# A table of position bias: eight copies of 128 rows within DRAM in place of one transfer from SBUF

## The chip, the cores and the metric

The kernel runs on one core of a Trainium2 chip. The core has a matrix engine (TensorE, PE in the profile), a vector engine (VectorE, DVE), an engine for activations and copies (ScalarE, ACT), a general one (GpSimd, POOL) and an engine that issues the transfers (SyncE, SP). Each engine works through its own list of instructions strictly in order and waits at an instruction until what it needs is there. Transfers between DRAM and the on-chip SBUF run on 16 DMA engines, behind the instruction that issues them.

The metric is the device time of one execution in microseconds. Three runs of the kernel before took 1793.67, 1798.79 and 1799.83 us; the median is 1798.79 us.

## The reference

Five layers run one after another on 512 tokens of width 1024: a latent attention (MLA), a sliding-window attention (SWA), an attention with forget gates (FOX), a second MLA, and then a block of another kind with four mixers, a feed-forward part and a gate. Only two places matter here. The last block adds a learned bias to the attention scores of eight heads, and that bias depends only on the distance between the two tokens:

```python
bias_tab[:, rel_bucket(tq[:, None] - spos[None, :])]     # 8 heads, 32 buckets, distances 0 to 511
```

And the second layer, SWA, is where the kernel happens to prepare it:

```python
x = first_block(...)          # layers MLA, SWA, FOX, MLA
x = second_block(x, ..., rel_bias_2, ...)
```

## The kernel before

Every matrix product is done in three passes over operands that are split into a high and a low part. A weight block comes from DRAM into a raw tile (`wr`, six buffers), ACT rounds it to the high part (`wh`, line 137), POOL subtracts to get the low part (`wl`, line 138), and PE multiplies with both (lines 156 to 158). A raw buffer is free for the next load when POOL has read it. All transfers are issued by SP, in one queue.

Inside one layer the work goes over pairs of heads. For each pair, `prep` projects queries and keys into PSUM banks (`ps_acc`, three of them), ACT and DVE split these into parts (line 225 to 227 for keys, 202 and 203 for queries) and so free the bank, and then two heads are scored, exponentiated and multiplied with the values. The second layer starts with a projection of its values, one gate, then keys and queries of the first pair together (`proj_multi`, 96 matmuls of 256 columns), then the next projection.

A scheduler sets the order of the instructions on each engine from the program and a model of their times. An instruction that is written late but has all that it needs can come to stand earlier in its engine's list.

Right behind the first layer, `rel_rows` makes a table of the bias: a one-hot matrix times the bias table gives one row of 640 numbers for each of the 8 heads (512 distances and a masked tail), in SBUF, on 8 partitions. Line 792 writes every row 128 times into a DRAM tensor `rel` of 8 x 128 x 640 numbers. Much later, in the last block, `rel_bias` (line 798) reads one head's 128 rows with a step of 639 numbers, so that each partition gets the row shifted by one: this turns a function of distance into a 128 x 512 bias tile. The first of these loads is issued at 1096.3 us.

Of the kernel before, what the change touches and what calls it, by code (L numbers as in the profile page):

```python
# [9 lines left out]
F32 = mybir.dt.float32  # L10
# [5 lines left out]
P, S, D, T = 128, 512, 1024, 4  # L16
# [59 lines left out]
class Act:  # L76


    def __init__(s, hi, lo, n):
        s.hi, s.lo, s.n = hi, lo, n  # L80
# [8 lines left out]
class Kern:  # L89
    def __init__(s, ctx, tc, I, C):  # L90
        s.tc, s.nc, s.I, s.C = tc, tc.nc, I, C
        s.ctx = ctx
        s.sb = ctx.enter_context(tc.tile_pool(name="sb", bufs=1))
        s.dram = ctx.enter_context(tc.tile_pool(name="dram", bufs=1, space=bass.MemoryType.DRAM))
        s.phase_pool, s.phase_tags = None, {}
        s.ps = ctx.enter_context(tc.tile_pool(name="ps", bufs=1, space=PSUM))
        nc = s.nc
        s.ident = s.const("c_ident")
        s.small = s.sb.tile([P, 8], F32, name="small")
        nc.vector.memset(s.small[:, 0:4], -0.5)  # L100
        nc.vector.memset(s.small[:, 4:5], 1e-6)
        nc.vector.memset(s.small[:, 5:6], 1.0)
        s.x = []
        s.step = 48

    def const(s, name, dt=F32):
# [538 lines left out]
    def swa(s, j, li, xT, g_next):  # L645
        nc, I = s.nc, s.I
        Win, Wo = I["swa_w_in"][j], I["swa_w_out"][j]
        sinks = s.bcast_row(I["swa_sinks"][j], "gq")
        vt = [s.t(g, [P, T, 2, 2, 64], R, name="v") for g in ("ckv", "cq")]
        s.v_proj(Win, 1280, 256, xT, lambda t, ps: s.v_split(ps, [v[:, t] for v in vt]))  # L650
        oT = s.act(8)
        K = {}

        def prep(p):
            kp, pr = divmod(p, 4)
            if p == 0:
                kps, qps = s.proj_multi([(Win, 1024, P, "acc"), (Win, 0, P, "acc")], xT)
            else:
                kps = s.proj(Win, 1024 + kp * P, P, xT) if pr == 0 else None
                qps = None  # L660
            if pr == 0:
                K[kp] = s.split_k(kps)
            win = s.t("rope", [P, 2, 256], name="win")
            nc.sync.dma_start(win, s.C["c_win"][p])
            qt = s.split_q(qps or s.proj(Win, p * P, P, xT))
            return qt, [k[:, pr // 2] for k in K[kp]], win

        def head(d, p, e):
            hd = 2 * p + e
            q, (kd, kl), win = d  # L670
            return s.attend(lambda out, i, k0: s.qk_mm(out, i, k0, q, e, kd, kl), [0, 0, 1, 2],
                            lambda i: win[:, e, 128:] if i == 0 else win[:, e], 0.125, s.vsel(vt[p // 4], (p % 4) // 2),
                            sink=sinks[:, hd:hd + 1])

        s.pairs(range(8), prep, head, Win, 1536, xT, oT)
        return s.layer_end(Wo, oT, li, g_next)

# [101 lines left out]
    def rel_rows(s):  # L779

        nc = s.nc
        hot = s.t("p", [32, S])
        nc.sync.dma_start(hot, s.C["c_hot"])
        tab = s.t("f", [32, 8])
        nc.sync.dma_start(tab, s.I["rel_bias_2"].rearrange("h b -> b h"))
        s.rel = s.dram.tile([8, P, 640], F32, name="rel")
        r = s.t("p", [8, 640])
        ps = s.p("acc")
        nc.tensor.matmul(ps[:8], tab, hot, start=True, stop=True)
        nc.vector.memset(r[:, 512:], NEG)  # L790
        nc.scalar.mul(r[:, :512], ps[:8], 8.0)
        nc.sync.dma_start(s.rel, r.rearrange("h (o c) -> h o c", o=1).to_broadcast([8, P, 640]))

    def rel_bias(s, h):


        b = s.t("rb", [P, S])
        s.nc.sync.dma_start(b, bass.AP(tensor=s.rel.tensor, offset=s.rel.offset + h * P * 640 + 127,
                                       ap=[[639, P], [1, S]]))
        return b  # L800

    def conv(s, W, hT, mix, b):
# [326 lines left out]
```

## Time and profile before

| | |
|---|---|
| median of three runs | 1798.79 us |
| the profiled execution | 1800.88 us |
| its span, first to last instruction | 1799.1 us |
| TensorE busy | 1695.6 us (94% of the span) |
| VectorE, ScalarE, GpSimd busy | 959.6, 873.9, 853.9 us |
| mean granted TensorE clock | 0.975 |
| share of the DMA engines' time in use | 34.7% |

The profile comes from one execution. The time of that execution is 1.8 us longer than its span, and 2.1 us above the median of the three runs. The engines' busy times overlap, so they do not add up to the span. The first layer ends and the second begins at about 275 us; the second ends at about 500 us.

### The profile page before, as it was taken

How to read it: one execution, taken by the hardware profiler on the slowest of the kernel's cores; microseconds unless marked ns; L12 is line 12 of the kernel's file. 1: busy time of each engine (PE TensorE's matmuls, PEld its weight loads, DVE VectorE, ACT ScalarE, POOL GpSimd, SP SyncE). 2: the span in 40 equal slices, each digit the busy share in tenths (PEclk: the TensorE clock that was granted, in tenths of full speed). 3: DMA queues.
4: the chain of work that ended last, by engine and by line, in shares of the span. 5: the costliest groups of instructions: out<-in, count | busy, mean ns of one | idle time of the engine just before them, and what ended most of it. 6: DMA issues, size and time to landing. Idle time of an engine off the chain costs nothing.

```text
span 1799.1 us, 25682 instructions
## 1 busy us (share of the span) xinstructions
PE 1695.6 (94%) x8818; PEld 1429.8 (79%) x8818; DVE 959.6 (53%) x2223; ACT 873.9 (49%) x2054; POOL 853.9 (47%) x775
## 2 busy tenths in 40 slices
PE   8999999499899999999999998999999999999999
PEld 7888778377788888877888777877788888888877
DVE  4587643278763575576477667499545222210054
ACT  4566533366635565662466653654544333332252
POOL 1645433234345565645644424635744444444571
PEclk9999999699899999999999999999999999999999
DMA  5534534422224233423354522332322333332321
GB/s 166 132 94 118 166 90 56 115 81 71 61 55 118 79 80 83 116 85 118 96 131 100 158 86 58 94 89 59 111 90 81 94 94 94 94 95 87 100 99 71
DMA packets 190203, 173.89 MB, mean 97 GB/s; under 512 B 14152, under 2 KB 154824, under 8 KB 190072
## 3 DMA queue, kind: packets, MB, share of 16 engines
q1 hardware_dynamic: 190072, 172.25, 34.7%
q8 instruction: 70, 1.15, 0.3%
q14 instruction: 61, 0.50, 0.1%
HBM read 148.31 MB, written 6.85 MB: 86 GB/s over the span
## 4 chain that ended last, share of the span: by engine, by line
PE 51%; DVE 9%; ACT 3%; POOL 2%; issue 2%; DMA 1%; SPq 0%; ACTq 0%; POOLq 0%; DVEq 0%
PE ps_acc L156 11%; PE ps_acc L157 10%; PE ps_acc L158 10%; PE ps_s L156 4%; PE ps_s L157 4%; PE ps_s L158 4%; PE ps_o L451 2%; PE ps_t L442 2%; DVE p L426 1%; ACT p L418 1%; DVE sel L918 1%; DVE m L917 1%; DVE p L402 1%; DVE ptl L184 1%; PE ps_s L237 1%
## 5 line engine op out<-in xcount | busy, mean ns | idle before, releaser
L138 POOL TENSOR_TENSOR wl<-wr,wh 128x512 fp32r<-128x512 f32 (+2 forms) x362 | 471.1, 1312 | 460.0 <-ACT wh L137 444.9
L137 ACT CAST wh<-wr 128x512 fp32r<-128x512 f32 (+2 forms) x368 | 223.5, 613 | 408.8 <-PE ps_acc L157 138.5
L156 PE MATMUL ps_acc<-act,wh 128*128 128x512 f32 (+1 forms) x880 | 335.8, 382 | 27.8 <-DVE qk L227 26.9
L157 PE MATMUL ps_acc<-act,wh 128*128 128x512 f32 (+1 forms) x880 | 334.3, 380 | 0.3 <-DVE act L184 0.2
L158 PE MATMUL ps_acc<-act,wl 128*128 128x512 f32 (+1 forms) x880 | 334.1, 380 | 0.0
L156 PEld LDWEIGHTS ps_acc<-act,wh 128*128 128x128 f32 x880 | 165.8, 188 | 58.6 <-issue 27.3
L158 PEld LDWEIGHTS ps_acc<-act,wl 128*128 128x128 f32 x880 | 165.5, 188 | 31.1
L157 PEld LDWEIGHTS ps_acc<-act,wh 128*128 128x128 f32 x880 | 166.0, 189 | 30.5 <-DVE act L184 0.7
L418 ACT ACTIVATE p<-p,st 128x256 f32<-128x256 f32 (+3 forms) x288 | 153.5, 537 | 30.0 <-DVE st L409 15.6
L156 PE MATMUL ps_acc<-wh,act 128*128 128x256 f32 (+3 forms) x384 | 131.8, 343 | 7.3 <-ACT act L468 3.1
L184 DVE TENSOR_TENSOR ptl<-ps_t,pth 128x512 fp32r<-128x512 f32 (+1 forms) x200 | 117.5, 597 | 38.1 <-ACT pth L183 37.2
L183 ACT CAST pth<-ps_t 128x512 fp32r<-128x512 f32 (+1 forms) x200 | 100.2, 516 | 75.2 <-PE ps_t L442 66.1
L426 DVE TENSOR_SCALAR p<-p,st 128x256 f32<-128x256 f32 (+3 forms) x264 | 132.7, 561 | 1.8
L442 PE MATMUL ps_t<-c_ident,p 128*128 128x128 f32 x672 | 117.5, 283 | 16.7 <-DVE p L426 12.5
L158 PE MATMUL ps_acc<-wh,act 128*128 128x256 f32 (+3 forms) x384 | 128.8, 336 | 0.1
L157 PE MATMUL ps_acc<-wl,act 128*128 128x256 f32 (+3 forms) x384 | 128.3, 334 | 0.0
L442 PEld LDWEIGHTS ps_t<-c_ident,p 128*128 128x128 f32 x672 | 82.3, 143 | 33.8 <-DVE p L426 14.0
L451 PE MATMUL ps_o<-pth,v 128*128 128x256 f32 (+3 forms) x288 | 90.0, 318 | 6.2 <-DVE og L462 4.2
L451 PE MATMUL ps_o<-ptl,v 128*128 128x256 f32 (+3 forms) x288 | 88.3, 335 | 4.8 <-DVE ptl L184 4.5
L156 PEld LDWEIGHTS ps_acc<-wh,act 128*128 128x128 f32 x384 | 75.9, 198 | 15.7 <-ACT act L468 3.3
L157 PEld LDWEIGHTS ps_acc<-wl,act 128*128 128x128 f32 x384 | 75.7, 197 | 5.1 <-issue 0.5
L158 PEld LDWEIGHTS ps_acc<-wh,act 128*128 128x128 f32 x384 | 75.3, 196 | 5.2 <-DVE act L184 0.3
(371 smaller groups left out, 3797.3 us busy)
## 6 DMA issues: line engine op xcount, KB each, us to landing
wr<-in_w_gate_up_dram SPq DMA_DIRECT2D x88, 256.0 KB, 2.9
wr<-in_fox_w_in_dram SPq DMA_DIRECT2D x60, 256.0 KB, 3.1
wr<-in_w_in_dram SPq DMA_DIRECT2D x48, 256.0 KB, 2.9
wr<-in_w_down_dram SPq DMA_DIRECT2D x44, 256.0 KB, 2.6
wr<-in_swa_w_in_dram SPq DMA_DIRECT2D x40, 256.0 KB, 3.1
wr<-in_mla_w_in_dram SPq DMA_DIRECT2D x32, 256.0 KB, 3.4
qk<-qk SPq DMA_DIRECT2D x32, 256.0 KB, 3.2
wr<-in_mla_w_out_dram SPq DMA_DIRECT2D x32, 256.0 KB, 3.7
```

What stands on the lines that cost most here:

```text
L137: nc.scalar.copy(h, raw)
L138: (nc.vector if dve else nc.gpsimd).tensor_sub(l, raw, h.bitcast(F32))
L156: mm(out, lh, rh, start=first, stop=False)
L157: mm(out, lh, rl, start=False, stop=False)
L158: return mm(out, ll, rh, start=False, stop=last)
L183: s.nc.scalar.copy(hi, src)
L184: s.nc.vector.tensor_sub(lo, src, hi.bitcast(F32))
L237: mm(out, q[:, e, c], kd[:, kk], start=True, stop=False)
L418: nc.scalar.activation(a, a, AF.Exp, bias=st[:, 1, i:i + 1], scale=scale, accum_out=st[:, 2, i:i + 1])
L426: nc.vector.tensor_scalar_mul(a, a, st[:, 3, i:i + 1])
L442: nc.tensor.transpose(ps[:, n:n + P], sc[:, c:c + P], s.ident)
L451: nc.tensor.matmul(o[:, j * P:j * P + m], vj, pp[:, c:c + m], start=first, stop=k == 1 and grp[-1] == max(2, grp[-1]) and j == grp[-1], sk ...
```

## The change

The row of each head is first written once to a small DRAM tensor `rel_row` (8 x 640). A new function `rel_spread` copies one head's row 128 times from there into that head's own DRAM tensor, so `rel` becomes eight tensors. It is called in `prep` of the second layer, once for each of the eight pairs of heads, behind the load of the window mask. `rel_bias` reads from the head's own tensor. The values in the table and all other instructions are the same.

```diff
@@ rel_rows, before line 786
-        s.rel = s.dram.tile([8, P, 640], F32, name="rel")
+        s.rel = [s.dram.tile([P, 640], F32, name="rel", tag=f"rel{h}") for h in range(8)]
+        s.rel_row = s.dram.tile([8, 640], F32, name="rel_row")
...
-        nc.sync.dma_start(s.rel, r.rearrange("h (o c) -> h o c", o=1).to_broadcast([8, P, 640]))
+        nc.sync.dma_start(s.rel_row, r)
+
+    def rel_spread(s, h):
+
+        row = s.rel_row[h]
+        s.nc.sync.dma_start(s.rel[h], bass.AP(tensor=row.tensor, offset=row.offset, ap=[[0, P], [1, 640]]))
@@ swa, prep
             win = s.t("rope", [P, 2, 256], name="win")
             nc.sync.dma_start(win, s.C["c_win"][p])
+            if s.rel:
+                s.rel_spread(p)
@@ rel_bias
-        s.nc.sync.dma_start(b, bass.AP(tensor=s.rel.tensor, offset=s.rel.offset + h * P * 640 + 127,
-                                       ap=[[639, P], [1, S]]))
+        s.nc.sync.dma_start(b, bass.AP(tensor=s.rel[h].tensor, offset=s.rel[h].offset + 127, ap=[[639, P], [1, S]]))
```

Line numbers of the changed kernel are higher by one in the first half of the file and by more behind `rel_rows`. The first place is SP's list at the start of the second layer, before. `rel` is the table, `p` the rows in SBUF, `cq` and `ckv` take the norm's gain and bias rows that the end of the second layer needs, and `wr` are weights of the second layer.

```order
L134 DMA wr_3418<-in_swa_w_in_dram 128x4x128
L792 DMA rel_3062<-p_3063 1024x1x640
L255 DMA cq_4979<-in_ln_g_dram 128x1024
L255 DMA ckv_4981<-in_ln_b_dram 128x1024
L134 DMA wr_3562<-in_swa_w_in_dram 128x4x128
L134 DMA wr_3580<-in_swa_w_in_dram 128x4x128
```

The same place in the changed kernel:

```order
L135 DMA wr_3428<-in_swa_w_in_dram 128x4x128
L796 DMA rel_row_3070<-p_3071 8x640
L801 DMA rel_3062<-rel_row_3070 128x640
L801 DMA rel_3063<-rel_row_3070 128x640
L801 DMA rel_3064<-rel_row_3070 128x640
L801 DMA rel_3065<-rel_row_3070 128x640
L801 DMA rel_3066<-rel_row_3070 128x640
L801 DMA rel_3067<-rel_row_3070 128x640
L801 DMA rel_3068<-rel_row_3070 128x640
L801 DMA rel_3069<-rel_row_3070 128x640
L256 DMA cq_4995<-in_ln_g_dram 128x1024
L256 DMA ckv_4997<-in_ln_b_dram 128x1024
```

One row has become nine, at the same place: all eight copies stand directly behind the write of `rel_row`, ahead of the two norm rows and of the second layer's later weights, and not beside the loads of the window masks, where the code calls them. SP waits at the first copy until `rel_row` has landed.

The second place is ACT's list where the second layer's first keys are split, in the changed kernel; `wh` are high parts of weights, `qk` parts of keys and queries.

```order
L605 ACTIVATE f_3262<-ps_acc_3225 128x512
L138 CAST wh_3575<-wr_3573 128x512
L138 CAST wh_3593<-wr_3591 128x512
L226 CAST qk_3387<-ps_acc_3289 64x512
L227 CAST qk_3387<-ps_acc_3289 64x512
L138 CAST wh_3731<-wr_3729 128x512
L208 CAST qk_3388<-qk_3388 64x512
```

Nothing has moved here: the lists of PE, DVE, ACT and POOL are the same as before but for line numbers and buffer numbers. Two weights (`wr_3573`, `wr_3591`, loaded behind the norm rows) are rounded ahead of the first split of the keys.

## Rows read from the trace of the kernel before

**Rows 1.** Page, part 2: busy tenths and granted clock in 40 slices of 45 us

```profile
PE   8999999499899999999999998999999999999999
PEclk9999999699899999999999999999999999999999
```

**Rows 2.** Waits of PE over the span: us in total, times, longest

```profile
PE ps_acc L156 <- DVE qk L227: 26.9, 1, 26.9
```

**Rows 3.** Timeline of PE: start us, us, instruction [idle before it, releaser]

```profile
297.21 0.28 PE L156 MATMUL ps_acc<-act,wh 128*128 128x256 f32 x1
...
308.40 0.28 PE L158 MATMUL ps_acc<-act,wl 128*128 128x256 f32 x1
...
313.88 0.39 PE L158 MATMUL ps_acc<-act,wl 128*128 128x512 f32 x1
341.13 0.77 PE L156 MATMUL ps_acc<-act,wh 128*128 128x512 f32 x1 [26.86 <-DVE qk L227]
341.69 0.63 PE L157 MATMUL ps_acc<-act,wh 128*128 128x512 f32 x1
...
345.10 0.63 PE L156 MATMUL ps_acc<-act,wh 128*128 128x512 f32 x1
```

**Rows 4.** Timeline of ACT and DVE, 297 to 341 us

```profile
297.75 0.59 ACT L604 ACTIVATE f<-ps_acc 128x512 f32<-128x512 f32 x1
335.21 0.62 ACT L137 CAST wh<-wr 128x512 fp32r<-128x512 f32 x1 [36.87 <-DMA wr<-in_swa_w_in_dram]
...
336.54 0.57 ACT L225 CAST qk<-ps_acc 64x512 fp32r<-64x512 f32 x1
...
340.29 0.69 DVE L227 TENSOR_TENSOR qk<-ps_acc,qk 64x512 fp32r<-64x512 f32 x1 [1.87 <-ACT qk L226]
```

**Rows 5.** Timeline of SP's issues, 275 to 330 us

```profile
276.99 0.81 SPq L792 DMA_DIRECT2D rel<-p  x1
283.01 0.35 SPq L255 DMA_DIRECT2D cq<-in_ln_g_dram  x1
285.38 17.05 SPq L255 DMA_DIRECT2D ckv<-in_ln_b_dram  x1
302.53 27.98 SPq L134 DMA_DIRECT2D wr<-in_swa_w_in_dram  x3
```

**Rows 6.** DMA view, 300 to 303 us: queue's packets, MB, share; issues, size, us to landing

```profile
q1 hardware_dynamic: 58, 0.15, 47.5%
...
wr<-in_swa_w_in_dram SPq DMA_DIRECT2D x1, 256.0 KB, 32.6
```

**Rows 7.** Windows: us, busy of PE, PEld, DVE, ACT, POOL, clock, DMA share, GB/s

```profile
298.00:302.00 4.00, 4.00 (x36) 4.00 (x35) 0.69 (x1) 0.34 (x1) 1.26 (x1) 1.00 0.47 49
...
332.00:334.00 2.00, 0.00 (x0) 0.00 (x0) 0.00 (x0) 0.00 (x0) 0.00 (x0) 0.50 0.88 307
...
344.00:346.00 2.00, 2.00 (x8) 1.61 (x7) 0.69 (x1) 1.10 (x2) 1.27 (x2) 0.50 0.45 120
346.00:348.00 2.00, 2.00 (x11) 1.69 (x11) 1.43 (x5) 0.62 (x1) 0.53 (x1) 0.95 0.67 185
...
380.00:400.00 20.00, 18.78 (x92) 15.56 (x93) 15.82 (x52) 13.87 (x37) 6.50 (x5) 0.91 0.22 61
```

**Rows 8.** DMA view over the span: issues, KB each, median us to landing

```profile
rel<-p SPq DMA_DIRECT2D x1, 2560.0 KB
...
x_dram<-x SPq DMA_DIRECT2D x4, 512.0 KB, 3.0
...
sel<-in_g_mix_post_dram SPq DMA_DIRECT2D x1, 512.0 KB, 3.8
...
forget<-f SPq DMA_DIRECT2D x1, 32.0 KB, 1.6
```

**Rows 9.** Timeline of POOL, 286 to 350 us

```profile
290.72 2.53 POOL L138 TENSOR_TENSOR wl<-wr,wh 128x512 fp32r<-128x512 f32 x2 [10.61 <-ACT wh L137]
...
297.97 1.28 POOL L138 TENSOR_TENSOR wl<-wr,wh 128x512 fp32r<-128x512 f32 x1 [0.17 <-ACT wh L137]
```

More of the change, by code (lines that the diff above doesn't have):

```diff
@@ L103, in __init__ @@
         s.x = []
+        s.rel = None
         s.step = 48
```

## The prediction

> **What bounds the kernel now.** I read the page first. TensorE is busy for 94% of the span, so I looked for the 6% that are missing. In the slices of 45 us one stands out, the eighth (315 to 360 us): four tenths busy, at a granted clock of six tenths [rows 1]. The list of PE's waits over the whole span names the place: one single wait of 26.9 us on DVE's key split, line 227 [rows 2]. The timeline of PE shows it between 313.88 and 341.13 us [rows 3].
>
> I then followed that wait back, engine by engine. DVE's second key split started at 340.29 us and needed ACT's copy. ACT had done its last piece of work at 297.75 us and stood still for 36.87 us at a cast, line 137, whose weights had not landed; the copies of the keys, line 225, stand behind that cast in ACT's list, although the keys themselves were long in PSUM [rows 4]. (They were ready at about 305.7 us: the 96 matmuls from 297.21 to 308.40 are 24 for keys, 24 for queries, 24 for keys, 24 for queries, at 0.118 us each [rows 3].) So a late weight on ACT's list held a PSUM bank, and the bank held PE.
>
> The weight was late because of the queue it stood in. SP issued the table `rel` at 276.99 us; the issue of the second norm row then took 17.05 us and the next three weight issues 27.98 us together [rows 5]. The weight issued at 302.53 us landed 32.6 us later, at 335.1 [rows 6]. In the middle of the transfer the DMA engines are 0.47 busy and move 49 GB/s [rows 7]; the table has 2560 KB, which is 2.62 MB [rows 8], and at 49 GB/s that is 53.5 us, about 278 to 331 us. Directly behind it, at 332 to 334 us, the same engines move 307 GB/s [rows 7]. So for 53 us one slow transfer stood ahead of everything else.
>
> **The change part by part.**
>
> What goes: the 53 us transfer. With it goes PE's standstill, if nothing else is late. PE's next matmul would start one spacing behind the one at 313.88, at 314.1 us; it started at 341.13. That is 27.0 us. [...] PE had not idled before 314 us, so I expect the clock to stay up.
>
> What comes: one write of 20 KB, eight copies, and one wait of SP at the first copy for `rel_row` to land. The nearest row for that write is the 32 KB one of the forget table, 1.6 us to landing [rows 8], so SP stands until about 279 us. Behind it on SP are the copies and the norm rows, which before were issued at 283.01 us, held by other work; eight issues at 0.35 to 0.81 us each [rows 5] end between 282 and 286 us. At worst the norm rows, which only the layer's end needs, are 3 us later. The first weight behind them cannot be issued before POOL has read a raw buffer, at about 292 us (two subtractions from 290.72 on; the last of the six buffers is free at 299.3) [rows 9]. So SP's new wait and its eight extra issues cost nothing.
>
> What is not in the trace is a copy within DRAM. The question is when the last of the eight ends; I call that E. Before, the table's end at about 331 us was followed by PE's return at 341.1 us, 10.1 us later (norm rows, two weights, their casts, the key splits). PE needs this by 314.1, so the stall is gone if E is up to 304 us, and above that it is E - 304 us.
> - From below: 2.62 MB at the 307 GB/s that the engines reach elsewhere [rows 7] are 8.5 us, E = 288 us.
> - From above: the old pace of 49 GB/s, 53.5 us, E = 333 us: no gain, 2 us lost.
> - Between them lie rows of either half of the work. A row of DRAM read for 128 partitions, 512 KB, lands in 3.8 us, and a write of 512 KB from SBUF to DRAM in 3.0 us [rows 8]. A copy of 320 KB should not take longer than the 3.8. Even eight of them one after another, without any overlap, are 30 us, E = 309 us, a stall of 5 us.
>
> I take the value near the lower end, E about 290 us: reading one DRAM row 128 times is the nearest row, and several transfers are in flight at once in this queue. What is late next is then not a transfer at all. ACT's two casts wait for PE to be done with the keys' weights (about 304.3 and 305.7 us), the four key copies and two DVE splits took from 336.54 to 340.98 us, 4.4 us, in the trace [rows 4], and so the bank is free at about 311 us, 3 us before PE asks for it.
>
> [...]
>
> Of the gain a little may be paid back: in 380 to 400 us PE idles 1.2 of 20 us on short waits [rows 7], and the stretch right behind the stall had fewer since weights had been loaded ahead. I put 0 to 1.5 us, and take 0.5.
>
> Sum: 27.0 + 2.5 - 0.5 = 29.0 us. From the profiled execution's 1800.88 us that gives 1771.9 us; that execution lies 2.1 us above the median of 1798.79, so against the median it is 1769.8. I predict 1770 us.
>
> **The rivals.**
> - *The copies are slower than I think, E between 305 and 315.* One after another, or together at 80 to 100 GB/s in place of 307. For it: each copy both reads and writes DRAM, and no row shows that. Against it: either half is fast. PE would stand 1 to 11 us, part of that again at half clock: 1772 to 1783 us.
> - *No change.* The slow part of the old transfer was not its source but writing rows of 2560 bytes; then the copies keep 49 GB/s, E = 333, and PE returns 2 us later than before: 1797 to 1802 us. Against it: the write of 512 KB to DRAM in 3.0 us.
> - *Slower.* Copying within DRAM runs below the old pace, because 128 reads of one short DRAM row and the writes meet in the same memory. It decides from E = 331 on, that is below about 50 GB/s. At half the old pace, 25 GB/s, the copies last 105 us, E = 385; the weights are stuck all that time, and PE returns at 395 us, 54 us later than before: 1853 us. Against it are the same two rows: both halves run far faster alone.
> - *The gain is handed back inside the second layer.* For it: DVE is busy 15.82 of 20 us at 380 to 400 us. Against it: PE is busy 18.78 there [rows 7], and during the stall no engine got ahead except for six raw weights. Half the gain lost would be 1784 us.
> - *The change does not do what it says.* It does not: the eight copies are not spread over the second layer but stand in one block where the old transfer stood. That alone costs nothing as long as the block is short, and by E = 290 it ends before the first weight behind it is asked for. It matters only in the rivals above, where a block is worse than copies with gaps between them.
>
> **How the numbers follow.** Forecast 0.80; slow copies 0.10; no change 0.04; slower 0.03; handed back 0.03. About 0.3%, 5.4 us, is what a measurement can tell from no change here. Faster by more: 0.80 + 0.10 + 0.03 = 0.93; within: 0.04; slower: 0.03. The forecast's own range is the 1 us of the pay-back, the 3 us by which E could pass 304 and some 4 us of scatter between runs (1793.67 to 1799.83): 1765 to 1776. The slow copies reach up to 1783; taking in the better half of them gives 1765 to 1778.
>
> **What would show it.** In the changed kernel's trace: nine issues of SP between 277 and 286 us; a DMA share well above 0.47 right behind them, and nothing of the copies left by 295 us; the weight issues short again, with landings of about 3 us; ACT's cast waiting for PE, not for a transfer; no wait of PE above some 3 us between 300 and 350 us; the clock at 1.00 through that stretch; a span near 1770 us. The prediction is wrong if the copies still run at 310 us, or if PE's wait has moved elsewhere in the second layer with 10 us or more.

## The result, and the profile after

The changed kernel takes 1772.18 us (median of 4 runs, 1771.13 to 1772.59); the kernel before takes 1799.31 us beside it. The ratio is 0.984 with a 95% interval of 0.982 to 0.987: 27.1 us faster. Forecast were 1770 us and a range of 1765 to 1778.

The page of the changed kernel, part 2, in 40 slices of 44 us: the hole in the eighth slice [rows 1] is gone, and so is its low clock.

```profile
PE   8999999999999999999999998999999999999999
PEclk9999999999999999989999999999999999999999
```

The waits of PE over the whole span (total, times, longest): the one wait of 26.9 us [rows 2] has left the list, which now begins with many short ones.

```profile
PE ps_t L443 <- DVE p L427: 13.3, 17, 2.5
```

The timeline of PE at the place where it stood still. In the kernel before, the projection behind the first keys and queries came 27 us late [rows 3]; here it follows at the next spacing.

```profile
314.43 0.39 PE L159 MATMUL ps_acc<-act,wl 128*128 128x512 f32 x1
314.67 0.40 PE L157 MATMUL ps_acc<-act,wh 128*128 128x512 f32 x1
314.90 0.39 PE L158 MATMUL ps_acc<-act,wh 128*128 128x512 f32 x1
```

The timelines of ACT and DVE ahead of it, to be held against [rows 4]. The cast ahead of the key copies waits 0.79 us for PE to be done with older weights, not for a transfer; the keys are split by 311.3 us, 3 us before PE needs the bank.

```profile
306.37 0.62 ACT L138 CAST wh<-wr 128x512 fp32r<-128x512 f32 x1 [0.79 <-PE ps_acc L158]
306.90 0.58 ACT L226 CAST qk<-ps_acc 64x512 fp32r<-64x512 f32 x1
...
310.65 0.69 DVE L228 TENSOR_TENSOR qk<-ps_acc,qk 64x512 fp32r<-64x512 f32 x1 [1.87 <-ACT qk L227]
```

The timeline of SP's issues. SP waits 1.2 us for the row to land and issues eight copies in 5 us. The first norm row follows at once: set against the start of the layer, which is 0.55 us later than before, the copies hold it back by 0.65 us. The second norm row is not held back, and the first weight is issued at 292.59 us, when POOL has read a raw buffer. The issues of 17 and 28 us [rows 5] are gone.

```profile
277.54 0.35 SPq L796 DMA_DIRECT2D rel_row<-p  x1
279.11 5.01 SPq L801 DMA_DIRECT2D rel<-rel_row  x8
284.21 0.58 SPq L256 DMA_DIRECT2D cq<-in_ln_g_dram  x1
285.93 0.34 SPq L256 DMA_DIRECT2D ckv<-in_ln_b_dram  x1
292.59 39.86 SPq L135 DMA_DIRECT2D wr<-in_swa_w_in_dram  x17
```

The DMA view from 270 to 300 us (size, median us to landing): a copy of 320 KB lands in 7.1 us with the others in flight, a weight in 3.2 us, where it was 32.6 [rows 6].

```profile
rel<-rel_row SPq DMA_DIRECT2D x8, 320.0 KB, 7.1
wr<-in_swa_w_in_dram SPq DMA_DIRECT2D x6, 256.0 KB, 3.2
```

Windows of the changed kernel (columns as in [rows 7]): the copies run on all engines at 292 GB/s in place of 49.

```profile
282.00:284.00 2.00, 2.00 (x18) 1.92 (x17) 1.69 (x2) 1.25 (x3) 0.00 (x0) 1.00 1.00 292
```

Where the gain goes from there can be followed with instructions that exist in both kernels. SP's timeline before, at the write of the forget table in the third layer and the first write of the residual behind it:

```profile
560.77 0.34 SPq L716 DMA_DIRECT2D forget<-f  x1
...
830.90 0.33 SPq L775 DMA_DIRECT2D x_dram<-x  x1
```

and after:

```profile
531.89 0.34 SPq L719 DMA_DIRECT2D forget<-f  x1
...
804.59 0.33 SPq L778 DMA_DIRECT2D x_dram<-x  x1
```

The first comes 28.9 us earlier, the second only 26.3, and the end of the span is 28.3 us earlier (1799.1 against 1770.8).

### The profile page after: what moved, and what is told of

It is laid out like the page before. It is cut to its first block, busy times and chain, and to the rows that moved or that the text cites. A ratio compares the mean times of both kernels' runs of the same rounds, so it can differ in the third digit from the quotient of the medians.

```text
span 1770.8 us, 25691 instructions
## 1 busy us (share of the span) xinstructions
PE 1693.8 (96%) x8818; PEld 1429.2 (81%) x8818; DVE 958.4 (54%) x2223; ACT 873.7 (49%) x2054; POOL 853.4 (48%) x775
## 4 chain that ended last, share of the span: by engine, by line
PE 52%; DVE 8%; ACT 2%; issue 2%; DMA 2%; POOL 2%; SPq 0%; ACTq 0%; POOLq 0%; DVEq 0%
PE ps_acc L157 11%; PE ps_acc L158 11%; PE ps_acc L159 11%; PE ps_s L158 4%; PE ps_s L157 4%; PE ps_s L159 4%; PE ps_o L452 2%; PE ps_t L443 2%; DVE p L427 1%; ACT p L419 1%; DVE sel L926 1%; DVE m L925 1%; DVE ptl L185 1%; DMA wr<-in_mla_w_in_dram 1%; DVE p L403 1%
```

## The experiments

The theory after the result was: the old transfer was slow because of where it read, its slowness made the weights late, and nothing else of the change matters. The rivals were that it was slow because few engines worked on it, that one large transfer holds a queue and eight small ones do not, and that the position of the copies in the program matters. Each kernel ran beside the kernel before, whose median was 1801 to 1803 us in these series.

**The changed kernel again**, as the yardstick.

> The changed kernel as it stands, beside the others on the same chip, as their yardstick. Expected 1772 us, PE without a wait above 3 us between 300 and 350 us, the eight copies landed by about 293 us.

It took 1769.0 us (1764.5 to 1773.8), ratio 0.982 (0.980 to 0.985). So what follows has to differ by more than some 5 us to mean anything by its time alone.

**The source alone.** One transfer as before, but from DRAM:

```diff
-        nc.sync.dma_start(s.rel, r ... .to_broadcast([8, P, 640]))
+        nc.sync.dma_start(s.rel_row, r)
+        nc.sync.dma_start(s.rel, bass.AP(tensor=s.rel_row.tensor, offset=s.rel_row.offset, ap=[[640, 8], [0, P], [1, 640]]))
```

> The source alone is changed: the rows are written to DRAM first, and then one transfer of 8 x 128 x 640 reads them from there. Theory 'source': the old transfer was slow because it read eight neighbouring SBUF partitions; from DRAM one transfer is fast even if it uses only half of the engines, about 120 to 150 GB/s, 17 to 22 us, over by about 302 us, no stall of PE, 1772 to 1775 us. Rival 'half of the engines': it was slow because a transfer whose outer dimension is 8 is spread over few engines at some 6 GB/s each; then this one takes 53 us like the old one, PE waits about 27 us, 1798 to 1802 us. Rival 'size': one transfer blocks and eight do not; 1798 us too.

1771.5 us, ratio 0.984 (0.982 to 0.985): the whole gain. Its window during the transfer shows half of the engines' time in use, as before, and four times the rate, more than the 120 to 150 GB/s that I had expected:

```profile
280.00:282.00 2.00, 1.92 (x18) 1.72 (x16) 2.00 (x4) 0.55 (x2) 0.00 (x0) 1.00 0.52 202
```

So neither the size of the old transfer nor the half of the engines' time that it left unused made it slow.

**The number alone.** Eight transfers, each from one partition of SBUF:

```diff
-        nc.sync.dma_start(s.rel, r ... .to_broadcast([8, P, 640]))
+        for h in range(8):
+            nc.sync.dma_start(s.rel[h] ..., r[h:h + 1] ... .to_broadcast([1, P, 640]))
```

> The number alone is changed: eight transfers of 128 rows, one head each, straight from SBUF as before, no row in DRAM. Theory 'source': each of them reads one partition through one place however many engines work on it; it gets no faster than the old one, more likely half its rate (25 to 30 GB/s in place of 49), so 53 to 105 us in all, PE waits 27 to 80 us, 1798 to 1853 us. Rival 'half of the engines': 128 rows spread over all engines, twice the old rate, about 27 us, over by 306 us, a stall of 2 us, 1772 to 1776 us. Rival 'size': as the changed kernel, 1772 us.

1847.9 us, ratio 1.026 (1.023 to 1.029): 47 us slower than the kernel before. Now 0.90 of all engines' time is in use, at 26 GB/s, and PE's longest wait is 57.9 us:

```profile
284.00:288.00 4.00, 4.00 (x37) 4.00 (x36) 2.42 (x6) 1.92 (x5) 0.00 (x0) 1.00 0.90 26
```

Twice the engines' time and half the rate: a busy share of 0.90 went with 26 GB/s here, and one of 1.03 with 393 GB/s in the next experiment, so the share does not tell the throughput. The profile does not name what the busy engines waited for; the two experiments that follow show that the rate hangs on where the source rows stand. Splitting by heads alone would have been a loss.

**SBUF as the source, spread out.** The matmul writes each row on 16 partitions, and one transfer reads all 128 (`wide` repeats each column of the bias table 16 times):

```diff
+        nc.vector.tensor_copy(wide ..., tab ... .to_broadcast([32, 8, 16]))
-        nc.tensor.matmul(ps[:8], tab, hot, start=True, stop=True)
+        nc.tensor.matmul(ps, wide, hot, start=True, stop=True)
...
+        nc.sync.dma_start(s.rel.rearrange("h (a b) c -> (h a) b c", b=8), r ... .to_broadcast([P, 8, 640]))
```

> The source stays in SBUF and the transfer stays one, but the eight rows stand 16 times each on all 128 partitions (the matmul writes them so), and each partition's row is written 8 times. Theory 'source': the reads are spread over all of SBUF, so the 2.62 MB go at 250 to 300 GB/s, 9 to 11 us, over by 290 us, no stall, 1771 to 1774 us. Rival 'size': one large transfer holds the queue, 1798 us. If SBUF as such were a slow source, more than 25 us and a stall.

1770.8 us, ratio 0.982 (0.980 to 0.985), with one transfer of 2.6 MB at 393 GB/s, no row in DRAM and no extra wait:

```profile
282.00:284.00 2.00, 1.45 (x12) 1.03 (x9) 1.65 (x5) 2.00 (x4) 0.02 (x1) 1.00 1.03 393
```

**The same eight rows, on partitions further apart.** As the kernel before, but each row is written on four partitions, and the transfer reads every fourth:

```diff
-        nc.sync.dma_start(s.rel, r.rearrange(...).to_broadcast([8, P, 640]))
+        nc.sync.dma_start(s.rel, r[0:32:4].rearrange(...).to_broadcast([8, P, 640]))
```

> One transfer from SBUF again, with the same shape, the same eight source rows and half of the engines, but the rows stand on partitions 0, 4, 8 to 28 in place of 0 to 7 (the matmul writes every row four times). Theory 'shared place': partitions that are neighbours share a way out of SBUF that gives 25 to 28 GB/s (27 GB/s for one partition at a time, 49 for eight neighbours); four apart each row has its own, so the transfer runs at 190 GB/s or so, like the one from DRAM on half of the engines, 14 us, no stall, 1769 to 1773 us. Rival 'few partitions': eight partitions read again and again are slow wherever they stand; 49 GB/s, 53 us, PE waits 27 us, 1796 to 1802 us.

1774.9 us (1767.3 to 1777.0), ratio 0.985 (0.982 to 0.988). The median lies 2 us above the range expected, which is within the scatter. The shape and the number of rows are those of before; only the distance of the rows differs, and the rate goes from 49 to 211 GB/s:

```profile
280.00:282.00 2.00, 1.69 (x16) 1.71 (x16) 1.58 (x4) 1.72 (x3) 0.00 (x0) 1.00 0.53 211
```

This settles the cause: it is where the rows stand. Eight neighbouring partitions gave 49 GB/s, eight partitions four apart 211. A way out of SBUF that neighbours share would explain this: one partition at a time gave 26 GB/s, so by these rates eight neighbours would have an estimated two such ways. That is my reading; the runs show the rates, and neither such a way nor which partitions would share one.

**The old transfer in another queue**, issued by ACT:

```diff
-        nc.sync.dma_start(s.rel, r ... .to_broadcast([8, P, 640]))
+        nc.scalar.dma_start(s.rel, r ... .to_broadcast([8, P, 640]))
```

> The kernel before with one edit: the old transfer, one, from SBUF, slow as ever, is issued by ACT and not by SP, so the weights do not stand behind it in the same queue. Theory: the stall came from the order in the queue; the table still takes about 53 us or a little more, but the weights pass it, PE does not wait, 1772 to 1776 us. Rival: the old transfer holds the engines themselves; then weights stay late (landing 10 to 30 us instead of 3), PE waits 10 to 27 us, 1785 to 1800 us.

1796.8 us, ratio 0.997 (0.996 to 0.999); PE still waits 23.6 of the 26.9 us:

```profile
PE ps_acc L156 <- DVE qk L227: 23.6, 1, 23.6
```

My theory of this run fell. The weights are issued early, from 292 us on, in a queue of their own, and still come late, at the end one in 12 us, as ACT's timeline shows:

```profile
320.92 0.62 ACT L137 CAST wh<-wr 128x512 fp32r<-128x512 f32 x1 [22.42 <-DMA wr<-in_swa_w_in_dram]
332.98 0.62 ACT L137 CAST wh<-wr 128x512 fp32r<-128x512 f32 x1 [11.45 <-DMA wr<-in_swa_w_in_dram]
```

In its DMA view from 310 to 320 us, q10 is ACT's queue with the table and q1 is SP's (packets, MB, share): the table moves on as before, and the weights get 0.23 MB, 23 GB/s.

```profile
q10 hardware_dynamic: 193, 0.49, 47.4%
q1 hardware_dynamic: 456, 0.23, 7.9%
```

So it is not the order in SP's queue alone: the slow transfer holds the engines. A weight of 256 KB is 512 packets (0.23 MB / 456 is about 512 bytes each), 32 for each of 16 engines if they are spread evenly. The slow packets, 193 in 10 us on an estimated 8 engines (47.4% of 16), take an estimated 0.41 us each. If each weight packet on those engines waits for one slow packet, a weight takes an estimated 32 x 0.41 = 13 us, near the 12 seen. The packet counts bear this out. From 310 to 315 us and from 320 to 325 us there are as many packets of weights as of the table, 96 and 97, then 96 and 96. From 315 to 320 us the weights have 264 more, about the half of a weight, which would be the part for the other engines. So on the table's engines they seem to pass one for one. From 320 to 325 us:

```profile
q10 hardware_dynamic: 96, 0.25, 47.7%
q1 hardware_dynamic: 96, 0.05, 3.2%
```

The profile does not say which engine a packet ran on; that these 96 ran on the table's engines is inferred from the counts.

**No copies at all**, as a floor:

```diff
-            if s.rel:
-                s.rel_spread(p)
...
-        ... bass.AP(tensor=s.rel[h].tensor, offset=s.rel[h].offset + 127, ap=[[639, P], [1, S]])
+        ... bass.AP(tensor=s.rel_row[h].tensor, offset=s.rel_row[h].offset, ap=[[1, P], [1, S]])
```

> The copies are left out: the bias tiles of the last block are read straight from the one row (with another shift, so the values of the bias are not the reference's). Theory: the eight copies and their wait cost nothing in the changed kernel, so this takes the same time, 1771 to 1773 us. Rival: the copies still delay weights or share bandwidth with them at the start of the second layer; then this is faster by 2 us or more.

1772.4 us, ratio 0.984 (0.982 to 0.986), as the changed kernel within the scatter. By the time alone a cost of 2 us, the rival's, could not be told from none. The traces say more: neither kernel has a wait of PE above 0.3 us between 270 and 350 us, and from the write of the row to that of the forget table it is 256.5 us without the copies and 254.4 with them. So the copies are hidden.

**The copies inside the second layer**, held to program order behind the loads of the masks:

```diff
-            nc.sync.dma_start(win, s.C["c_win"][p])
+            s.tc.keep_in_program_order(nc.sync.dma_start(win, s.C["c_win"][p]))
...
-        s.nc.sync.dma_start(s.rel[h], ...)
+        s.tc.keep_in_program_order(s.nc.sync.dma_start(s.rel[h], ...))
```

> The eight copies are held to their place in the program, one behind each load of a window mask: two stand at the start of the second layer and six inside it. Theory: in a block or spread, the copies are hidden; 1771 to 1774 us. Rival: inside the layer they stand ahead of weights that are needed soon and cost some us each, 1778 us or more; or the block at the start still costs something and spreading them gains 2 us.

1768.9 us, ratio 0.983 (0.981 to 0.985). The eight issues now reach from 276.1 to 422.5 us, and the time is the changed kernel's within its scatter (2 us below the range expected): one block or spread out, it makes no difference that can be measured.

**More copies**, to find the slack. Each copy is followed by one or three others into tensors that nobody reads:

```diff
+        for i in range(n - 1):          # n = 2 and n = 4
+            x = s.dram.tile([P, 640], F32, name="rel_extra", ...)
+            s.nc.sync.dma_start(x, bass.AP(tensor=row.tensor, offset=row.offset, ap=[[0, P], [1, 640]]))
```

> Every copy is made twice, the second into a tensor that nobody reads: 16 copies, 5.2 MB. By the prediction's formula a stall of PE begins when the last copy ends later than 304 us, and lasts E - 304. At the 280 GB/s seen in the changed kernel they end at about 299 us: no stall, 1772 us. Rival: any byte ahead of the weights delays PE; then 9 us of added transfer cost up to 9 us.

> Every copy is made four times: 32 copies, 10.5 MB, at 280 GB/s over by about 318 us. By the formula PE waits about 14 us, and comes back for some us at half clock: 1785 to 1789 us, with PE's wait again on the key split of DVE. Rival: transfers are hidden anyway and the old stall had another cause; then 1772 us.

Twice: 1769.7 us, no stall, though the engines are 0.91 to 1.06 busy from 284 to 308 us. The spare time is nearly used up there: ACT's cast stands 7.32 us for its weight, until 307.44 us, and PE still does not wait. Four times: 1789.7 us, and the old wait is back, on the same line, for 11.2 us:

```profile
PE ps_acc L157 <- DVE qk L228: 11.2, 1, 11.2
```

The expected 14 us of wait were not met, because the scheduler put the weights between the last copies, so "the end of the last copy" no longer says when the weights land. The threshold itself is thus bracketed, not measured: 16 copies cost nothing that shows. With 32 the write of the forget table comes 18.2 us later than in the changed kernel, from a start of the layer 1.0 us earlier: 11.2 us of this are the wait on the keys, 3.3 us a second wait of PE, on a query copy of ACT (line 203), and most of the rest is half clock: (1 - granted clock) adds up to 15.3 us in this layer against 5.1 in the changed kernel, and only 3.4 of them fall into the 11.2 us of waiting.

## Why the prediction was right, and where not

- *The stall of 27.0 us goes.* It did: PE's next matmul is at 314.67 us instead of 341.13, 26.5 us earlier, and the layer had begun 0.55 us later. The late chain from the weight over ACT's cast and the key split to PE's bank is confirmed by the run with 32 copies, which brings it back.
- *The 2.5 us of the sum.* No run shows this term; in its place the traces show 2.4 us of half clock. In the kernel before, PE came back at half clock, from 341.13 to about 346.2 us [rows 7], and matmuls of 512 columns were 0.426 us apart there [rows 3]; in the changed kernel they are 0.235 us apart, and the clock is 1.00 from 276 to 332 us. Of the 5.1 us that is an estimated 2.3. Measured are 2.4: the same matmul of the first scores is at 346.17 us in the kernel before and at 317.34 us in the changed one, 28.8 us earlier.

```profile
346.17 0.29 PE L238 MATMUL ps_s<-qk 128*128 128x256 f32 x1
...
317.34 0.28 PE L239 MATMUL ps_s<-qk 128*128 128x256 f32 x1
```

- *0.5 us paid back in the layer, and the rival that the gain is handed back there.* Not seen. The write of the forget table in the third layer is 28.9 us earlier, as much as that matmul; from a start 0.55 us later this is 29.4 us. (In between the lead goes up to 31.4 us near 482 us and down again by 495, while each kernel has stretches at half clock of its own.)
- *The copies end at about 290 us.* The last was issued at 283.5 and landed 9.0 us later, 292.5 us, with the norm rows in between. The value near the lower bound was right, and the estimate for copies one after another (309 us) was too late, since the copies overlap (eight issued within 4.4 us, a median of 7.1 us each to landing): reading one DRAM row 128 times and writing it within DRAM ran at 292 GB/s, near the 307 taken as the bound.
- *SP's new wait and eight extra issues cost nothing.* The first copy was issued at 279.11 us (forecast 279), the first weight at 292.59 (292); the 0.65 us by which the first norm row is held back cost PE nothing, which takes its next matmul at 314.67 us without a wait.
- *The rival on slow copies, the one on no change, and the slower one* all hung on the rate within DRAM, and the 292 GB/s exclude them. A slower outcome of their kind did exist, 1848 us, but for a split that kept SBUF as the source.
- *The change does not spread the copies over the layer.* So it was, and spreading them makes no measurable difference.
- *The weight was late because of the queue it stood in.* This step, in the reading of the profile, was incomplete. The run on ACT's queue shows that the weights are late in another queue too: 3.3 of the 26.9 us are won. The number came out right because the change takes away the slowness and not the order. From 310 to 330 us 23 GB/s were left to them there, beside the table's 49.
- *What made the old transfer slow?* The forecast needed only that copies within DRAM are fast. The share of the engines' time differs (0.47 in the old transfer, 0.52 from DRAM in one transfer, 1.00 in eight), but it is not the cause: at shares of 0.52 and 0.53 the table still went at 202 GB/s from DRAM and at 211 from SBUF. The cause is where the rows stand: 49 GB/s from eight neighbouring partitions, 26 from one at a time, 211 from eight that are four apart.
- *1770 us.* The 1772.2 us lie 2 us from it, but the changed kernel alone scatters from 1764.5 to 1773.8 us. That the sum is right to 2 us is partly luck; what bears it out are the leads within one execution, 26.5, 28.8 and 28.9 us.

What the forecast did not have are 2.7 us that were lost again at the start of the fourth layer, the second MLA. SP issues the layer's first weights 29.1 us earlier than before (763.89 against 792.95 us), but a row of its norm only 26.3 us earlier (792.38 against 818.70). PE has the same wait of 3.1 us there in both kernels, but only in the changed one does it run at half clock behind it. The windows at that place, before:

```profile
812.00:816.00 4.00, 4.00 (x18) 3.28 (x19) 0.64 (x1) 0.44 (x1) 1.29 (x1) 1.00 0.14 37
```

and after:

```profile
783.20:787.20 4.00, 4.00 (x10) 3.13 (x10) 0.38 (x1) 0.18 (x1) 1.27 (x1) 0.50 0.13 37
```

In the same 4 us, 10 matmuls are done and not 18. Another 2.0 us came back before the end, and these are not of the clock: from 819 to 1034 us of the kernel before, where the lead grows to 28.6 us, it is 1.00 in both kernels, and PE idles 4.6 us in this stretch in place of 6.4. Why its short waits are shorter was not traced.

## What to carry to other kernels

A transfer that stands out by a low rate at a steady busy share of the DMA engines is worth more attention than its bytes: look at what it reads, and above all at whether a broadcast reads a few neighbouring partitions of SBUF again and again (49 GB/s here). Put the rows apart (211 GB/s) or on many partitions (393), or pass through DRAM (202 in one transfer, 292 in eight), before thinking about splitting or moving the transfer; splitting it by partition made it 47 us worse, and another queue gave back 3.3 of the 26.9 us of waiting. When a wait is traced back to "a late transfer", test whether it is late because of its place in the queue or because the engines are held: here, where they were held, another queue cured little.

## What the runs showed of the hardware that was not expected

**Part of the scatter between runs is half clock.** For each profiled execution I added up (1 - granted clock) over its full windows of 10 us; the incomplete one at the end is left out. This is at most what full clock would have saved: where PE stands still the clock costs nothing, and matmuls of 512 columns came every 0.426 us at half clock [rows 3] against 0.235, which is not quite twice. Taking the sum from the span leaves numbers within 5.2 us of each other for the kernels without the stall, although their spans differ by up to 10.7 us:

| kernel | span, us | lost to the clock | rest |
|---|---|---|---|
| changed | 1770.8 | 30.6 | 1740.2 |
| changed, again | 1762.6 | 22.3 | 1740.3 |
| one transfer from DRAM | 1771.8 | 34.2 | 1737.6 |
| 128 partitions | 1771.2 | 34.5 | 1736.7 |
| rows four apart | 1773.3 | 32.5 | 1740.8 |
| no copies | 1770.6 | 32.6 | 1738.0 |
| 16 copies | 1765.9 | 24.0 | 1741.9 |
| inside the layer | 1765.2 | 27.2 | 1738.0 |

For the kernel before, 44.4 us are lost, 11.2 of them (22.3 us at half clock from 318.8 to 341.1) while PE stood still anyway; 1799.1 - 27.0 - 33.2 = 1738.9 us, a rest in the same range. So to within these 5 us the stall and the clock are the whole difference between the two kernels.

Over all 30 runs of these kernels, with each run's span and mean clock, the relation is looser. The spans lie between 1762.6 and 1775.2 us and the rests between 1731.5 and 1742.5 us; the standard deviation falls only from 2.8 to 2.4 us, and over 28 runs of the kernel before from 3.0 to 2.0. So half clock behind short waits is a part of the differences of a few us among the fast versions, and the rest stays open. What decides at a given place whether the clock falls, with the same wait of 3.1 us, these runs do not show.

**A second queue gave no way past the slow transfer.** With the table on ACT's queue, SP's weights got 23 GB/s from 310 to 330 us, while the table kept its 49; by the packet counts (96 and 96 from 320 to 325 us) one packet of weights went for each slow packet on the table's engines.
